# One transformer layer with routed experts, one core: the g2 row on VectorE, the first loads reordered, and g2's broadcast buffer lent to an expert load

## The chip, the cores and the metric

One core of a Trainium2 chip runs the program. It has five engines with queues of their own: TensorE (PE in the profile; its weight loads are PEld), VectorE (DVE), ScalarE (ACT), GpSimd (POOL) and SyncE (SP), which here only issues DMAs. The metric is device microseconds (us) of one execution, the median of several.

## The reference, cut to what matters

One layer of a decoder on 256 tokens of width 2048. A conditioning vector `c` gives six rows of 2048 numbers, `mod = silu(c) @ ada_w + ada_b`, split into `sh1, sc1, g1, sh2, sc2, g2`. Then

```
h = rmsnorm(x) * norm1_g * (1 + sc1) + sh1
x = x + g1 * (mixer(h))          # w_in (2048 x 5392), attention, gated delta rule, w_out (2048 x 2048)
h = rmsnorm(x) * norm2_g * (1 + sc2) + sh2
x = x + g2 * (moe(h))            # 32 experts, two per token; each a gated MLP 2048 -> 512 -> 2048
out = rmsnorm(x) * final_norm_g
```

All in float32. The weights are some 570 MB, each read once.

## The kernel before, in words

**Loads.** Every weight comes in pieces of 128 x 2048 float32 (1 MB, 8 KB in each partition) through one `Stream`, called `st` (its `pump`, `done` and `grow` are lines 122 to 160). The stream has a list of loads in a fixed order and a set of slots, tiles named `ring`. A load is issued on SyncE's queue into the next free slot; when a piece has been used, `done` frees its slot for the next load of the list. `grow` adds slots, `retire` takes a slot out once its present load has been used. At the start there are five slots (`main`, three, and `side`, two) and four borrowed ones (`spare`), which go back at the end of the w_in stage. When the buffers of the mixer are closed, four more come (`rb`), after the second half of w_out three (`rd`) and two (`yh`, `yl`, for one load each), and after routing two (`h20`, `h21`).

**The order of work.** The program is written in one order; a planner that simulates the engines then sets the order of the instructions on each engine, keeping the dependences. The stages are:

1. Start (lines 166 to 241). `c` is loaded and turned into columns. The conditioning rows sc1 and sh1 are made in slices (`ada_tile`, products on PE into a bank named `prow`). Before any product with w_in can run, x must be in, its mean square known (squares on ScalarE, line 518; reciprocal root; spread over columns as `rb`, line 529), and the modulated transpose `hx` made (lines 321 to 350) from `mod`, which needs small rows of `norm1_g` and `ada_b` (`crow`). SyncE issues x (four loads), then the five slots of the ring, then six small loads and the 128 KB of `wbr` (line 225), then the four spare slots.
2. w_in, by slices of its rows (`win_tile`, `win_pair`). Each piece is split into a high and a low part (`split`: ScalarE casts, line 289; VectorE or GpSimd subtracts, line 290) and three products are made of them.
3. The fill: attention and the delta rule (`delta`, `attention`), with w_in's last columns and the rows g1, sh2, sc2, g2 laid between them by `tick`. A row takes 16 pieces of ada_w (`row_tile`, lines 424 to 453). For g1, sh2 and g2 (i = 0, 1, 3) PE makes four products of 512 columns per piece, into a bank `prow`; for sc2 (i = 2) VectorE multiplies the piece by its column of silu(c) and adds it to a running sum `racc`, two instructions of 128 x 1024 per piece (line 441; the first piece line 439), and four products at the end sum over partitions. The results are added to `mrow` (line 450).
4. w_out in two halves (`wout_part`, four parts each). The first eight pieces of g2's row are read in the fill, the last eight in the first half, two after each part. In the second half each part also spreads 512 columns of g2 over the partitions (two products with `identr`, a copy by ScalarE, line 1036) into `g2b`, a tile of 8 KB per partition that lives to the end.
5. Routing (lines 1052 to 1154): a chain of short VectorE instructions from the logits to the one-hot matrices `oh`.
6. The experts, two at a time. For each, eight pieces of gate and up weights (`hidden`: products `u` on PE) and four of down weights (`second`: products `d`, then VectorE scales by the gate and `g2b`, line 1232). `scatter` adds the result to x. 384 pieces in all.
7. The final norm and the stores.

Of the kernel before, what the change touches and what calls it, by code (L numbers as in the profile page):

```python
# [50 lines left out]
def hybrid_moe(ctx: ExitStack, tc: tile.TileContext, x, c, norm1_g, norm2_g, early, ada_w, ada_b, w_bb,  # L51
# [118 lines left out]
    cols, crows, start_loads = {}, {}, []  # L170
    for nk, r in ((4, 4), (2, 8)):
        w = P * nk
        rows = crows[nk] = tmp.tile([P, 2, 256], F32, name="crow", tag="ct", bufs=2).rearrange("p u t -> p (u t)")[0:3 * r, 0:w]
        for i, row in enumerate((norm1_g[0, 0:r * w], ada_b[0, 0:r * w], ada_b[0, D:D + r * w])):
            start_loads.append((rows[i * r:(i + 1) * r], row.rearrange("(j n) -> j n", n=w)))
# [43 lines left out]
    spare = [(wk, "Tm"), (wk, "qk"), (cst, "h20"), (cst, "h21")]  # L219
    for n in range(4):  # L220
        nc.sync.dma_start(x1[n], xin[n])
    st.grow(*main, *side)
    wbr = tmp.tile([P, 2, 384], F32, name="wbr", tag="pT").rearrange("p u s -> p (u s)")[:, 0:16 * KT]
    for a in start_loads + [(wbr, w_bb)]:
        nc.sync.dma_start(*a)
    st.grow(*spare)

    for nk, r in ((4, 4), (2, 8)):
# [6 lines left out]
        for k0, n in SLICES:  # L235
# [4 lines left out]
           .bitcast(F32R).rearrange("p (k n) -> p k n", n=16) for i in range(2)]  # L240
    wbr = wbr.rearrange("p (k n) -> p k n", n=16)
# [50 lines left out]


# [130 lines left out]
    def row_tile(i, kt):  # L424
        def on_pe(t):
            if kt == 0:
                rowp[i] = bank("r", name="prow2")
            for g in range(4):
                mm(rowp[i][32 * g:32 * g + 32, :], csil[:, kt, 3 - i:35 - i], t[:, 512 * g:512 * (g + 1)],
                   start=(kt == 0), stop=(kt == 15))  # L430

        def on_dve(t):
            if kt == 0:
                rowp[i] = wk.tile([P, D], F32, name="racc", tag="racc")
            acc = rowp[i]
            for h in range(2):
                c = slice(1024 * h, 1024 * (h + 1))
                if kt == 0:
                    V.tensor_scalar(acc[:, c], t[:, c], csil[:, kt, 3:4], None, op0=ALU.mult)
                else:  # L440
                    V.scalar_tensor_tensor(acc[:, c], t[:, c], csil[:, kt, 3:4], acc[:, c], op0=ALU.mult, op1=ALU.add)
            if kt == 15:
                rowp[i] = bank("d", name="prow2")
                for g in range(4):
                    mm(rowp[i][32 * g:32 * g + 32, :], onec[:, 3 - i:35 - i], acc[:, 512 * g:512 * (g + 1)])

        def f(t):
            (on_dve if i == 2 else on_pe)(t)
            if kt == 15:
                V.tensor_tensor(mrow, mrow, rowp.pop(i), op=ALU.add)  # L450
                if i == 2:
                    V.scalar_tensor_tensor(n2row, mrow, 1.0, n2row, op0=ALU.add, op1=ALU.mult)
        return f
# [76 lines left out]
    S.copy(wbb[0], wbr)  # L530
    V.tensor_tensor(wbb[1], wbr, wbb[0], op=ALU.subtract)
# [476 lines left out]
    g2b = ring2.tile([P, D], F32, name="g2b")  # L1008
# [22 lines left out]
    for n in range(4):  # L1031
        ns = slice(512 * n, 512 * (n + 1))
        wout_part(n, (1, 2), g1hl, ep.tile([P, 512], F32, name="g1s", tag="ak0"))
        pg = bank("w")
        spread2(pg, g1hl, 3, n)
        S.copy(g2b[:, ns], pg)
# [4 lines left out]
        for b in range(NB):  # L1041
# [8 lines left out]
            S.activation(y, x1[n][:, b], AF.Square, accum_out=ss2[:, b, n:n + 1])  # L1050
    r2 = cst.tile([P, NB], F32, name="r2")
# [22 lines left out]
    g2h = g2b.rearrange("p (n h j) -> p n h j", n=4, h=2)  # L1074
# [141 lines left out]
    def second(u, hT, gs, ys, st, n0, m, yl=None, at=None):  # L1216
# [13 lines left out]
        for h, q in ((u, slice(0, 64)), (1 - u, slice(64, 128))):  # L1230
            o = z[q, 0:256 * m] if yl else ys[h][q, c]
            V.scalar_tensor_tensor(o.rearrange("p (n j) -> p n j", n=m), pd[q, 0:256 * m].rearrange("p (n j) -> p n j", n=m),  # L1232
                                   gs[q, h, u:u + 1], g2h[q, n0:n0 + m, h], op0=ALU.mult, op1=ALU.mult)
# [69 lines left out]
    behind = []  # L1303
    for e in range(0, NE, 2):
# [8 lines left out]
        hid.append(hidden(2 * a + 1, now.xg, st))  # L1313
# [166 lines left out]
```

## Time and profile before

| | us |
|---|---|
| median of three runs | 1624.28 (1623.28 to 1625.85) |
| the profiled execution | 1624.69 |
| its span, first to last instruction | 1622.9 |

The page gives the busy time of each engine (PE 1521.0, DVE 732.8, ACT 400.4, POOL 184.0), the span in 40 slices, the DMA queues, the chain that ended last, and the costliest groups of instructions with the idle time before them and what ended it. The trace can be asked for instructions in order of time, for the busy time of any stretch, and for waits. Busy time of PE is modelled for pipelined products: a PE that is shown busy all through may still have room; the starts of its weight loads (PEld) show how densely it issues. A row like `473.48 1.86 PEld ... x16 [0.84 <-issue]` says that 16 weight loads began at 473.48 us, after 0.84 us in which PE issued nothing and no semaphore is known to have held it.

### The profile page before, as it was taken

Reading aid. Unit: us, or ns where it says so; the run is one execution under the profiler, and the core shown is the slowest. Engines: PE = TensorE matmul, PEld = TensorE weight load, DVE = VectorE, ACT = ScalarE, POOL = GpSimd, SP = SyncE. Lnnn points to the kernel's source line nnn. Section 1 sums busy time; section 2 is a strip of 40 time slices with the busy share of each in tenths; the row PEclk is TensorE's granted clock in tenths of the full one; section 3 lists DMA queues with packets and bytes.
Section 4 is the critical chain, followed back from the end, with each engine's and each line's share of the span. In section 5 each row is a group of like instructions: output and inputs, shape, how many; then the busy total and the mean of one; then the engine's idle time right before and its main releaser. Section 6 shows DMA issues by size and latency. Waiting matters only on the chain. (4 is left out here: it accounts for less than half of the span.)

```text
span 1622.9 us, 23431 instructions
## 1 busy us (share of the span) xinstructions
PE 1521.0 (94%) x9852; PEld 926.3 (57%) x9852; DVE 732.8 (45%) x1201; ACT 400.4 (25%) x691; POOL 184.0 (11%) x103
## 2 busy tenths in 40 slices
PE   5999999999999999899999999999999999999895
PEld 3778877678776677445445445455445435445433
DVE  3544587487624544333443443344235225325325
ACT  4333366444443344120110110111011101101103
POOL 1111223234333241000000000000000000000001
PEclk8999999999999999899999999999999999999998
DMA  9977654888857374799999999999999999999995
GB/s 377 408 300 290 216 224 178 349 316 320 312 216 291 144 305 180 281 410 420 392 420 420 421 421 420 421 420 420 420 421 421 420 421 421 421 420 420 422 420 223
DMA packets 81412, 573.74 MB, mean 354 GB/s; under 512 B 9740, under 2 KB 10100, under 8 KB 12312
## 3 DMA queue, kind: packets, MB, share of 16 engines
q1 hardware_dynamic: 81272, 572.20, 87.4%
q8 instruction: 79, 1.29, 0.3%
q14 instruction: 29, 0.24, 0.0%
q10 hardware_dynamic: 32, 0.01, 0.0%
HBM read 570.07 MB, written 2.10 MB: 353 GB/s over the span
## 5 line engine op out<-in xcount | busy, mean ns | idle before, releaser
L67 PE MATMUL u<-ring,xg 128*64 128x512 f32 x2048 | 483.7, 602 | 7.5 <-DMA ring<-in_expert_gu_dram 7.3
L67 PEld LDWEIGHTS u<-ring,xg 128*64 128x64 f32 x2048 | 134.4, 136 | 235.7 <-issue 190.7
L67 PE MATMUL d<-ring,hidT 128*64 128x256 f32 x2048 | 239.1, 384 | 12.0 <-DMA ring<-in_expert_dn_dram 8.6
L67 PE MATMUL w<-hx,stg 128*128 128x256 f32 x1440 | 191.0, 288 | 7.4 <-ACT hx L349 2.8
L67 PEld LDWEIGHTS d<-ring,hidT 128*64 128x64 f32 x2048 | 144.1, 137 | 93.1 <-issue 10.6
L67 PEld LDWEIGHTS w<-hx,stg 128*128 128x128 f32 x1440 | 177.9, 191 | 32.8 <-issue 10.9
L290 POOL TENSOR_TENSOR stg<-ring,stg 128x1024 fp32r<-128x1024 f32 x50 | 121.9, 2439 | 373.0 <-ACT stg L289 273.4
L289 ACT CAST stg<-ring 128x1024 fp32r<-128x1024 f32 x116 | 121.3, 1047 | 164.3 <-PE w L67 140.9
L1248 DVE TENSOR_TENSOR xt<-xt,s 128x512 f32<-128x512 f32 x120 | 82.5, 687 | 159.2 <-PE s L67 158.4
L1235 ACT CAST yh<-z 64x512 fp32r<-64x512 f32 (+1 forms) x132 | 78.8, 597 | 279.2 <-DVE z L1232 274.3
L1232 DVE SCALAR_TENSOR_TENSOR z<-d,gs,g2b 64x512 f32<-64x512 f32 (+1 forms) x132 | 95.8, 726 | 84.0 <-PE d L67 81.8
L290 DVE TENSOR_TENSOR stg<-ring,stg 128x1024 fp32r<-128x1024 f32 x66 | 91.4, 1385 | 65.2 <-ACT stg L289 65.0
L67 PE MATMUL prow<-ring,csil 128*32 128x512 f32 (+1 forms) x768 | 102.3, 565 | 13.8 <-DMA ring<-in_early_dram 13.5
L1337 POOL TENSOR_TENSOR xf<-xt,fgb 128x1024 f32<-128x1024 f32 x3 | 7.0, 2359 | 953.1 <-DVE xf L1232 953.1
L1165 DVE TENSOR_TENSOR xg<-g,sh2c 128x512 f32<-128x512 f32 x64 | 43.6, 690 | 136.8 <-PE u L67 76.2
L67 PEld LDWEIGHTS s<-yh,wt 128*128 128x128 f32 x240 | 45.4, 189 | 96.4 <-issue 60.4
L1204 ACT ACTIVATE hid<-u 64x512 f32<-64x512 f32 x32 | 18.9, 590 | 317.4 <-PE u L67 300.8
L1236 DVE TENSOR_TENSOR yl<-z,yh 64x512 fp32r<-64x512 f32 (+1 forms) x132 | 87.3, 661 | 5.1 <-ACT yh L1235 1.5
L67 PE MATMUL s<-yh,wt 128*128 128x256 f32 x240 | 75.6, 335 | 9.1 <-ACT yh L1235 5.0
L67 PE MATMUL w<-stg,hx 128*128 128x256 f32 x576 | 81.1, 291 | 0.7 <-DVE ak L271 0.7
L1205 DVE TENSOR_TENSOR hid<-hid,u 64x512 f32<-64x512 f32 x32 | 22.1, 690 | 129.8 <-ACT hid L1204 129.6
L67 PEld LDWEIGHTS w<-stg,hx 128*128 128x128 f32 x576 | 71.1, 189 | 13.2 <-issue 9.8
(396 smaller groups left out, 1590.4 us busy)
## 6 DMA issues: line engine op xcount, KB each, us to landing
ring<-in_expert_gu_dram SPq DMA_DIRECT2D x256, 1024.0 KB, 19.8
ring<-in_expert_dn_dram SPq DMA_DIRECT2D x128, 1024.0 KB, 19.8
ring<-in_early_dram SPq DMA_DIRECT2D x90, 1024.0 KB, 8.2
ring<-in_ada_w_dram SPq DMA_DIRECT2D x64, 1024.0 KB, 6.4
xt<-in_x_dram SPq DMA_DIRECT2D x8, 512.0 KB
out_dram<-xt SPq DMA_DIRECT2D x8, 256.0 KB, 3.9
fgb<-in_final_norm_g_dram SPq DMA_DIRECT2D x1, 1024.0 KB
rw<-in_router_w_dram SPq DMA_DIRECT2D x1, 320.0 KB, 5.1
```

The lines of the kernel that those rows point to most:

```text
L67: return T.matmul(o, lhsT, rhs, start=start, stop=stop, skip_group_check=True)
L289: S.copy(hi, src)
L290: (G if nsplit[0] % GS[part] == GS[part] - 1 else V).tensor_tensor(lo, src, hi, op=ALU.subtract)
L1165: V.tensor_tensor(self.xg[:, 2 * q:2 * q + 2, 0:w], p[:, 0:2 * w].rearrange("p (k s) -> p k s", k=2), sh2c.rearrange("p n k -> p (n k)")[: ...
L1204: S.activation(hid[64:128], p[0:64], AF.Silu)
L1205: V.tensor_tensor(hid[0:64], hid[64:128], p[64:128], op=ALU.mult)
L1232: V.scalar_tensor_tensor(o.rearrange("p (n j) -> p n j", n=m), pd[q, 0:256 * m].rearrange("p (n j) -> p n j", n=m), gs[q, h, u:u + 1], g2h ...
L1235: S.copy(ys[h][q, c], o)
L1236: V.tensor_tensor(yl[h][q, c], o, ys[h][q, c], op=ALU.subtract)
L1248: V.tensor_tensor(x1[n][:, b], x1[n][:, b], p, op=ALU.add)
L1337: G.tensor_tensor(xf[n // 2][:, n % 2], x1[n], fgb[:, None, 512 * n:512 * (n + 1)].to_broadcast([P, NB, 512]), op=ALU.mult)
```

## The change

Three things are changed.

- The start. The five slots of the ring are filled first, then the four loads of x are issued, then the four spare slots. The six small rows and `wbr` are issued on ScalarE's queue, the rows at the very start, into buffers named `t2`; the split of `wbr` into its two halves is written earlier.
- g2's row. Its 16 pieces take the path that sc2's take: 32 instructions on VectorE into `racc`, and four products at the end.
- g2's spread. The tile `g2b` is no longer filled in the second half of w_out. After that half its slot is given to the stream for one load and then retired; during the second expert the tile is made in the same place and filled by `spread_g2`, four times two products and one copy, one after each of the last four pieces of that expert. The high and low halves of the row are made before routing ends, in the two buffers of `z`.

```
@@ start
+        rows = crows[nk] = scratch(w, 3 * r)
+        S.dma_start(rows[0:r], norm1_g[0, 0:r * w].rearrange("(j n) -> j n", n=w))
...
+    st.grow(*main, *side)
     for n in range(4):
         nc.sync.dma_start(x1[n], xin[n])
-    st.grow(*main, *side)
-    wbr = tmp.tile([P, 2, 384], F32, name="wbr", tag="pT").rearrange("p u s -> p (u s)")[:, 0:16 * KT]
-    for a in start_loads + [(wbr, w_bb)]:
-        nc.sync.dma_start(*a)
     st.grow(*spare)
...
+    S.dma_start(wbr, w_bb)
...
+    S.copy(wbb[0], wbr)
+    V.tensor_tensor(wbb[1], wbr, wbb[0], op=ALU.subtract)
@@ row_tile
-            (on_dve if i == 2 else on_pe)(t)
+            (on_dve if i >= 2 else on_pe)(t)
@@ second half of w_out
-        pg = bank("w")
-        spread2(pg, g1hl, 3, n)
-        S.copy(g2b[:, ns], pg)
...
+    st.grow((ring2, "g2b"))
+    st.retire((ring2, "g2b"))
@@ experts
+    g2hl = halves(*(mp.tile([P, 512], F32R, name="g2hl", tag="z") for _ in range(2)), mrow)
+    def spread_g2(n):
+        if n == 0:
+            assert not any(x == (ring2, "g2b") for _, x in st.tiles)
+            g2t.append(ring2.tile([P, D], F32, name="g2b", tag="g2b"))
+        p = bank("s", 1)
+        spread2(p, g2hl, 3, n)
+        S.copy(g2t[0][:, 512 * n:512 * (n + 1)], p)
...
-        hid.append(hidden(2 * a + 1, now.xg, st))
+        hid.append(hidden(2 * a + 1, now.xg, st, [] if e else [lambda: None] * 4 + [lambda n=n: spread_g2(n) for n in range(4)]))
```

## Rows read from the trace of the kernel before

**Rows 1.** The page of the profile: its first line, and of the 40 slices of the span (40.6 us each) the granted clock of PE and the busy share of the DMA engines, in tenths.

```profile
span 1622.9 us, 23431 instructions
...
PEclk8999999999999999899999999999999999999998
...
DMA  9977654888857374799999999999999999999995
```

**Rows 2.** Busy time by stretch (start:end, length, busy us and instructions of each engine, granted clock, share of the 16 DMA engines, GB/s), in the expert stage: its first long stretch (those after it up to 1580 read the same: share 1.01, 420 to 421 GB/s).

```profile
760.00:1000.00 240.00, 232.26 (x1418) 117.61 (x1419) 93.56 (x144) 27.38 (x45) 0.00 (x0) 0.99 1.01 415
```

**Rows 3.** The same view in stretches of 5 us, around the start of the expert stage.

```profile
625.00:630.00 5.00, 5.00 (x22) 3.53 (x20) 4.40 (x7) 2.51 (x6) 0.02 (x1) 1.00 0.00 0
...
655.00:660.00 5.00, 2.43 (x10) 2.33 (x11) 2.79 (x14) 0.00 (x0) 0.00 (x0) 0.50 0.96 400
...
660.00:665.00 5.00, 5.00 (x28) 4.64 (x28) 1.69 (x3) 1.39 (x2) 0.00 (x0) 0.64 0.04 11
...
695.00:700.00 5.00, 5.00 (x26) 2.29 (x24) 1.56 (x11) 0.20 (x1) 0.00 (x0) 1.00 1.02 433
```

**Rows 4.** Instructions in order of time (start, length, engine, line, operation, tensors, count, idle time before it and what ended it), SyncE's queue of DMA issues in the first 35 us.

```profile
2.62 2.44 SPq L186 DMA_DIRECT2D ring<-in_early_dram  x5
...
20.52 11.55 SPq L186 DMA_DIRECT2D ring<-in_early_dram  x11
```

**Rows 5.** Busy time by stretch of 4 us in the first 30 us.

```profile
0.00:4.00 4.00, 0.28 (x1) 0.18 (x1) 1.68 (x8) 1.59 (x2) 1.60 (x9) 1.00 0.54 165
...
8.00:12.00 4.00, 1.36 (x16) 0.68 (x16) 0.98 (x5) 2.94 (x8) 0.00 (x0) 1.00 1.01 428
...
20.00:24.00 4.00, 3.36 (x34) 2.40 (x35) 1.12 (x4) 0.78 (x2) 0.00 (x0) 1.00 0.66 223
```

**Rows 6.** Instructions in order of time, all engines, between the squares of x and the first products with w_in.

```profile
8.75 0.61 ACT L518 ACTIVATE t<-xt 128x512 f32<-128x512 f32 x1
...
11.21 0.48 DVE L526 TENSOR_SCALAR t<-ident,rs 128x128 f32<-128x128 f32 x2
...
25.52 1.99 ACT L289 CAST stg<-ring 128x1024 fp32r<-128x1024 f32 x2 [3.21 <-DMA ring<-in_early_dram]
...
26.60 1.23 DVE L290 TENSOR_TENSOR stg<-ring,stg 128x1024 fp32r<-128x1024 f32 x1 [2.70 <-ACT stg L289]
...
27.74 0.15 DVE L321 TENSOR_TENSOR mod<-d,cols 128x4 f32<-128x4 f32 x1
...
31.24 7.86 PE L67 MATMUL w<-hx,stg 128*128 128x256 f32 x48
```

**Rows 7.** What PE waited for between 31 and 100 us (the whole answer: us in total, times, longest).

```profile
PE w L67 <- ACT hx L349: 2.8, 1, 2.8
PE w L67 <- DVE hx L350: 0.5, 1, 0.5
```

**Rows 8.** Costliest groups between 440 and 580 us: PE's products for the rows on TensorE (busy us, mean ns of one). Of these 136 records 8 belong to another row and 128 to g2's (64 products, two records each).

```profile
L67 PE MATMUL prow<-ring,csil 128*32 128x512 f32 x136 | 22.1, 602 | 0.3 <-DMA ring<-in_ada_w_dram 0.3
```

**Rows 9.** Weight loads on PE in order of time: the first, one of the middle and the last of the fourteen bursts of g2's products, each with the row that follows it.

```profile
459.32 0.15 PEld L67 LDWEIGHTS prow<-ring,csil 128*32 128x32 f32 x6
460.31 0.74 PEld L67 LDWEIGHTS d<-t,Um 128*128 128x128 f32 x6 [0.84 <-DVE stg L290]
...
522.82 0.16 PEld L67 LDWEIGHTS prow<-ring,csil 128*32 128x32 f32 x8 [0.33 <-issue]
524.50 0.97 PEld L67 LDWEIGHTS d<-t,Um 128*128 128x128 f32 x8 [1.52 <-PE prow L67]
...
566.99 0.14 PEld L67 LDWEIGHTS prow<-ring,csil 128*32 128x32 f32 x4 [0.25 <-issue]
567.97 0.30 PEld L67 LDWEIGHTS w<-stg,aq 128*128 128x128 f32 x2 [0.84 <-issue]
```

**Rows 10.** The instructions that touch racc, the running sum of the sc2 row, which VectorE keeps today (count: shortest/median/longest ns, first and last start), and PE's weight loads that close such a row, with the row that follows.

```profile
L441 DVE SCALAR_TENSOR_TENSOR racc<-ring,csil,racc x30: 1255/1276/3402, 317.2 to 432.9; 128x1024 f32<-128x1024 f32 x30
```

```profile
455.55 0.16 PEld L67 LDWEIGHTS prow<-racc,onec 128*32 128x32 f32 x8
456.54 0.52 PEld L67 LDWEIGHTS a<-kswap,cq 64*128 64x128 f32 x4 [0.84 <-issue]
```

**Rows 11.** Busy time of all engines from 440 to 570 us, and of line 290 (the splits) alone.

```profile
440.00:570.00 130.00, 124.35 (x777) 89.21 (x777) 55.41 (x85) 48.93 (x92) 39.74 (x21) 0.97 0.61 227
```

```profile
440.00:570.00 130.00, 13.27 (x9) 22.39 (x9) 0.97 0.61 227
```

**Rows 12.** VectorE and GpSimd in order of time, two pairs: line 852 alone and line 852 beside a GpSimd split.

```profile
316.57 0.69 DVE L852 TENSOR_TENSOR Um<-ident,Um 128x512 f32<-128x512 f32 x1
...
322.85 2.51 DVE L852 TENSOR_TENSOR Um<-ident,Um 128x512 f32<-128x512 f32 x1
```

```profile
322.00 2.81 POOL L290 TENSOR_TENSOR stg<-ring,stg 128x1024 fp32r<-128x1024 f32 x1
```

**Rows 13.** Weight loads on PE around the first of the four spreads of g2 in the second half of w_out.

```profile
587.59 3.09 PEld L67 LDWEIGHTS w<-stg,bv 128*128 128x128 f32 x14 [0.36 <-issue]
591.04 0.29 PEld L67 LDWEIGHTS w<-g1hl,identr 32*128 32x128 f32 x2 [0.36 <-issue]
591.70 2.17 PEld L67 LDWEIGHTS w<-stg,bv 128*128 128x128 f32 x10 [0.36 <-issue]
```

**Rows 14.** PE in order of time in the routing stage: its wait for VectorE.

```profile
656.79 1.03 PE L67 MATMUL t<-Ae,before 128*128 128x32 f32 x4 [6.46 <-DVE Ae L1107]
```

More of the change, by code (lines that the diff above doesn't have):

```diff
@@ L168, in hybrid_moe @@
     S.dma_start(craw, c[0].rearrange("(k p) -> k p", p=P))
-    cols, crows, start_loads = {}, {}, []
+    cols, crows = {}, {}
     for nk, r in ((4, 4), (2, 8)):
         w = P * nk
-        rows = crows[nk] = tmp.tile([P, 2, 256], F32, name="crow", tag="ct", bufs=2).rearrange("p u t -> p (u t)")[0:3 * r, 0:w]
-        for i, row in enumerate((norm1_g[0, 0:r * w], ada_b[0, 0:r * w], ada_b[0, D:D + r * w])):
-            start_loads.append((rows[i * r:(i + 1) * r], row.rearrange("(j n) -> j n", n=w)))
+        rows = crows[nk] = scratch(w, 3 * r)
+        S.dma_start(rows[0:r], norm1_g[0, 0:r * w].rearrange("(j n) -> j n", n=w))
+        S.dma_start(rows[r:2 * r], ada_b[0, 0:r * w].rearrange("(j n) -> j n", n=w))
+        S.dma_start(rows[2 * r:3 * r], ada_b[0, D:D + r * w].rearrange("(j n) -> j n", n=w))
     V.memset(csil, 0.0)
@@ L240, in hybrid_moe @@
            .bitcast(F32R).rearrange("p (k n) -> p k n", n=16) for i in range(2)]
+    wbr = tmp.tile([P, 2, 384], F32, name="wbr", tag="pT").rearrange("p u s -> p (u s)")[:, 0:16 * KT]
+    S.dma_start(wbr, w_bb)
     wbr = wbr.rearrange("p (k n) -> p k n", n=16)
@@ L529, in hybrid_moe @@
     V.tensor_copy(rb, pt[:, 0:256])
-    S.copy(wbb[0], wbr)
-    V.tensor_tensor(wbb[1], wbr, wbb[0], op=ALU.subtract)
     use(first[3:CP])
@@ L1007, in hybrid_moe @@
     st.grow(*slots(ring2, "rb", R2))
-    g2b = ring2.tile([P, D], F32, name="g2b")
     h2hi, h2lo = ([ring2.tile([P, D], F32R, name=f"{n}{b}") for b in range(NB)] for n in ("h2hi", "h2lo"))
@@ L1073, in hybrid_moe @@
     psum = ctx.enter_context(tc.tile_pool(name="mps", bufs=1, space=bass.MemoryType.PSUM, reuse_waits="tile"))
-    g2h = g2b.rearrange("p (n h j) -> p n h j", n=4, h=2)
+    g2hl = halves(*(mp.tile([P, 512], F32R, name="g2hl", tag="z") for _ in range(2)), mrow)
+    g2t = []
     def small(name, shape, dt=F32):
@@ L1232, in second @@
             V.scalar_tensor_tensor(o.rearrange("p (n j) -> p n j", n=m), pd[q, 0:256 * m].rearrange("p (n j) -> p n j", n=m),
-                                   gs[q, h, u:u + 1], g2h[q, n0:n0 + m, h], op0=ALU.mult, op1=ALU.mult)
+                                   gs[q, h, u:u + 1], g2t[0].rearrange("p (n h j) -> p n h j", n=4, h=2)[q, n0:n0 + m, h], op0=ALU.mult, op1=ALU.mult)
             if yl:
```

## The prediction

> **What bounds the kernel now.** I read the page first, then stretches, then single waits. The page's DMA row says 9 almost throughout from the eighteenth slice on and much less before it [rows 1]. In the expert stage the stretch view shows the 16 DMA engines at a share of 1.01 [rows 2]: they never rest, so one piece (1.049 MB at 420 GB/s) costs 2.50 us whatever the engines do. In stretches of 5 us that state begins near 695 us [rows 3]. Before it the DMA engines pause: 0.00 at 625 to 630 us and 0.04 at 660 to 665 us, with PE shown busy all through. There every slot of the ring is full and PE decides when one comes free. So the end is the time at which the DMA engines become saturated, plus the bytes left over 420 GB/s, plus a tail that the change doesn't touch. Two things shorten it: a microsecond less on PE's path before 695 us counts once, and a piece brought in during a pause counts 2.50 us.
>
> PE's path reaches far back. From 31 to 100 us PE's products waited 3.3 us in all, none of it for a load [rows 7]. Its clock stands at 8 or 9 tenths in all slices [rows 1], so there is little to win from that.
>
> The sums are made against the profiled execution, 1624.69 us (span 1622.9 and 1.8 around it), 0.4 above the median of the runs.
>
> **The start.** PE's first product with w_in is at 31.24 us [rows 6]. It was not x that was late: the last squares began at 8.75 and the roots were spread by 11.69 (11.21 and 0.48). It was the first piece of w_in. It is sixth in the list (five pieces of ada come first), so it has the first spare slot, and SyncE issues that only at 20.52, behind the small loads and `wbr` [rows 4]; the DMA engines stood at 0.66 from 20 to 24 us against 1.01 before [rows 5]. The cast of that piece waited 3.21 us for it, and its subtraction (26.60 to 27.83) sat ahead of `mod` on VectorE; from `mod` (27.74) to the first product passed 3.50 us [rows 6].
>
> After the change five pieces and x, 5.24 + 2.10 = 7.34 MB, come first. At 428 GB/s [rows 5] that is 17.2 us, and with the 2 us that the DMA engines lose in the first 4 (share 0.54) x is there at 19 to 20 us. One more square (0.61) and the chain from the squares to the roots (9.36 to 11.69, 2.33 us) [rows 6] give 23; the same 3.50 us give 26.5. The first w_in piece lands 1.05 MB after x, near 22, and its cast and subtraction (1.99 + 1.23) end at 25.2. That is 4.7 us sooner than 31.24. The small loads on ScalarE's queue cost its idle time only, as long as x is what ScalarE waits for. Ends: +5 if all of that comes, -2 if x, which now has no slack, is late and the subtraction again goes ahead of `mod` (that order cost 3.6 us). I take 3, since the work on VectorE is the same and only one of the two delays is surely gone. By rows 7 there is no load wait behind it that would swallow the gain.
>
> **g2's row.** PE gives up 64 products, 128 records of the 136 that took 22.1 us [rows 8]. What they hold of PE's issue is read from the weight loads: from the first load of a burst to the next other load. There are fourteen bursts, 0.99 us in the first (459.32 to 460.31), 0.98 in the last (566.99 to 567.97), 19.7 us in all [rows 9]. Eight of them, 9.6 us, lie between attention and delta products until 492; three, 5.4 us, in the tail of the delta rule (510 to 525), where PE waits for VectorE anyway: after that at 522.82 PE still idled 1.52 us [rows 9]. Of these I count the last at nothing and half of the rest, 1.8. The three in the first half of w_out, 4.7 us, count fully. Against them stand four closing products, 0.99 us by those of sc2's row [rows 10]. Net 9.6 + 1.8 + 4.7 - 1.0 = 15.1 us.
>
> VectorE takes 32 instructions of 1.276 us, 40.8 us [rows 10]. From 440 to 570 us it is busy for 55.4 of 130 [rows 11], so they fit: 96 of 130. But the queue is in order. Behind each sit subtractions whose result PE needs, and a piece's slot is free only when both of its instructions are done; SyncE's queue is in order too, so everything behind that slot waits, w_out's pieces included. Some 85 VectorE instructions run in that window [rows 11]; each finds a row instruction ahead with a chance of 41/130 and waits half of 1.28 us, 0.2 us, together 17 us. Four staging buffers stand between VectorE and PE; I let a quarter, 4 us, through. So 11 us. Ends: 15 (none gets through) and -25 (all 40.8 us in PE's way, the 15.1 saved).
>
> The row shows a second price. Line 852 takes 0.69 us alone and 2.51 us when a GpSimd subtraction (322.00 to 324.81) runs beside it [rows 12]; of the 32 existing row instructions the longest took 3.40 us [rows 10]. The Trainium skill, SBUF — State Buffer, section "Who interferes with whom", says that a VectorE instruction with two inputs in SBUF and a GpSimd instruction that reads SBUF share one read interface, and whichever comes second is held until the first is through; rows 12 agree. By that rule the row's gain is what the first rival below makes of it. The median of 1.276 says that most row instructions escape it.
>
> **g2's spread and its buffer.** In w_out's second half each spread holds PE's issue from 590.68 (587.59 + 3.09) to 591.70, 1.02 us, of which 0.1 would be spent anyway [rows 13]. Four times 0.9 is 3.6 us on a PE that is busy throughout (ends 2 and 4.1). The same products now run in the second expert, near 695 us, when the DMA engines are the limit: nothing, and if that cover failed, the same 3.6 back.
>
> The lent slot lets one more piece in while the DMA engines would pause (660 to 665 us, 0.04 [rows 3]): 2.5 us. Ends 0 (its issue comes in order behind loads that wait for the routing) and 2.5. The new halves of the row put one VectorE instruction of 512 columns, about 0.69 us as line 852 [rows 12], near the routing chain, for which PE waits 6.46 us [rows 14]. I take 0.5 lost, ends 0 and 1.
>
> **Sum.** 3 + 11 + 3.6 + 2.5 - 0.5 = 19.6 us; 1624.69 - 19.6 = 1605.1, against the median 1604.7. I say 1605.
>
> **Rivals.**
> One: VectorE and GpSimd hold each other up. GpSimd is busy 39.7 us of the 130, nine splits of 22.4 us among it [rows 11]. If each of the nine waits for a whole row instruction (1.28), 11.5 us come back on the path of PE, and the row gives nothing net. Then 3 + 3.6 + 2.5 - 0.5 = 8.6, that is 1616. For: rows 12. Against: the median of rows 10.
>
> Two, slower: the row makes VectorE the bound. It has 130 - 55.4 = 74.6 us free there. At 3.40 us each 32 instructions need 109 and the stage grows by 34; less the other parts' 8.6 the kernel would stand near 1650, at a mean of 3.0 (96) at 1637. It decides from 32 d = 74.6 + 8.6, a mean d of 2.6 us. For: some run at twice the median, and SyncE's queue passes a late slot on to all loads. Against: the median, and that VectorE is free more than half of the time.
>
> Three: the start and the slot don't do what they say: x's lateness takes the place of the late w_in piece, and the lent slot's load is issued too late. Then 11 + 3.6 - 0.5 = 14.1, 1610.6. For: -2 to 5 at the start is wide. Against: rows 4 and 5.
>
> Four: everything comes at its better end but for what cannot: 4.7 + 15.1 + 3.6 + 2.5 = 25.9, 1599. For: VectorE's free time. Against: its in-order queue.
>
> Five: the planner lays the engines' order anew and loses elsewhere what is won: 1624.
>
> **How the numbers follow.** The forecast 0.37 (its own range 1601 to 1609), rival one 0.18, two 0.13, three 0.15, four 0.10, five 0.07. 0.2%, 3.2 us, is about what a measurement of this kernel can tell from no change. Faster: 0.37 + 0.18 + 0.15 + 0.10 = 0.80; same 0.07; slower 0.13. The range holds the forecast and rivals one, three and four with some room, 1594 to 1622; it leaves out rivals two and five, 0.20.
>
> **What would show it.** Right: the first w_in product near 27 us; no `prow` products after the g1 and sh2 rows but two closing groups of four; 32 more instructions at line 441 with a mean under 1.6 us; the second half of w_out shorter by 3 to 4 us; the DMA engines saturated some 20 us sooner than 695; 420 GB/s from there on. Wrong: PE waiting for `stg` from VectorE or GpSimd between 455 and 570; a mean over 2 us at line 441; SyncE waiting for `racc`; the first w_in product at 31 us or later; a stage of experts that isn't shifted but stretched.

## The result, and the profile after

The changed kernel takes 1634.29 us (median of six runs, 1630.63 to 1636.18), the kernel before, on the same chip, 1624.53 (1623.26 to 1626.68). The ratio is 1.0058, 95% interval [1.0048, 1.0068]: slower by 9.4 us. The forecast was 1605 with a range of 1594 to 1622, and 0.13 for slower. The execution that was profiled is the slowest of the six, 1636.18.

The page of the changed kernel, its first line, the granted clock and the DMA share of the 40 slices, to be read beside [rows 1]:

```profile
span 1634.4 us, 23238 instructions
...
PEclk8999999999998899799999999999999999999998
...
DMA  9987564888766374799999999999999999999995
```

The clock has a new dent in the thirteenth and fourteenth slices (490 to 572 us), within the stretch where the time went. I followed landmarks through both traces. The first product with w_in came later (31.24 to 33.31 us), the closing products of sc2's row earlier (455.55 to 454.81). From there to the high half of the g1 row, the first thing behind the first half of w_out, the kernel before took 124.8 us (455.55 to 580.30) and the changed one 136.5 (454.81 to 591.3). Of those 11.7 us it won 2.3 back by the first one-hot matrix of the routing, and lost 2.8 from there to the end. These are single executions; what the parts are worth is taken from the runs below.

Busy time by stretch (length, busy us and instructions of PE, PEld, DVE, ACT and POOL, granted clock, DMA share, GB/s), first of the kernel before, then of the changed one.

```profile
460.00:480.00 20.00, 20.00 (x154) 13.91 (x151) 6.20 (x14) 8.77 (x23) 5.82 (x3) 1.00 0.71 257
480.00:500.00 20.00, 20.00 (x162) 16.05 (x161) 6.26 (x8) 9.81 (x15) 8.61 (x4) 1.00 0.97 378
...
520.00:540.00 20.00, 15.82 (x72) 11.82 (x73) 16.08 (x25) 4.72 (x8) 3.47 (x4) 0.83 0.40 152
```

```profile
460.00:480.00 20.00, 17.67 (x147) 16.45 (x146) 20.00 (x21) 7.71 (x20) 5.18 (x3) 1.00 0.74 267
480.00:500.00 20.00, 14.26 (x103) 11.89 (x102) 20.00 (x18) 11.46 (x20) 14.10 (x4) 0.98 1.01 410
520.00:540.00 20.00, 11.27 (x34) 8.28 (x33) 16.79 (x25) 2.90 (x5) 2.59 (x3) 0.58 0.31 106
...
760.00:1000.00 240.00, 231.48 (x1378) 117.87 (x1374) 92.81 (x145) 27.38 (x45) 0.00 (x0) 0.98 1.00 407
```

For 40 us VectorE has no gap at all, where it had been busy for 12.5, and PE, which had been busy throughout, is idle for 8. From 520 to 540 us PE works 11.3 us of 20 instead of 15.8, and its granted clock is 0.58 instead of 0.83, close to the lower of its two levels (1.2 of 2.4 GHz). The last line answers to [rows 2]: 407 GB/s against 415.

What PE and SyncE waited for between the two landmarks in the changed kernel (engine, line, releaser: total, times, longest):

```profile
PE w L67 <- POOL stg L291: 6.9, 6, 4.3
PE w L67 <- DVE stg L291: 6.4, 2, 4.4
PE d L67 <- DVE t L909: 6.2, 2, 5.5
...
SPq L190 <- DVE racc L444: 23.3, 5, 8.4
```

All of these stood in the prediction's list of what would show it wrong, but for the third: PE waits 6.2 us for a step of the delta rule.

### The profile page after: what moved, and what is told of

Same layout as the page of the kernel before. It is cut to its first block, busy times and chain, and to the rows that moved or that the text cites. A ratio compares the mean times of both kernels' runs of the same rounds, so it can differ in the third digit from the quotient of the medians.

```text
span 1634.4 us, 23238 instructions
## 1 busy us (share of the span) xinstructions
PE 1515.8 (93%) x9732; PEld 933.5 (57%) x9732; DVE 774.0 (47%) x1234; ACT 401.4 (25%) x693; POOL 188.5 (12%) x103
## 5 line engine op out<-in xcount | busy, mean ns | idle before, releaser
L1166 DVE TENSOR_TENSOR xg<-g,sh2c 128x512 f32<-128x512 f32 x64 | 43.7, 690 | 126.4 <-PE u L67 71.1
L444 DVE SCALAR_TENSOR_TENSOR racc<-ring,csil,racc 128x1024 f32<-128x1024 f32 x60 | 87.7, 1494 | 7.7 <-DMA ring<-in_ada_w_dram 7.7
L67 PE MATMUL prow<-ring,csil 128*32 128x512 f32 (+1 forms) x640 | 82.0, 553 | 0.3 <-DVE csil L182 0.3
```

Of the source, the lines that this page charges most:

```text
L67: return T.matmul(o, lhsT, rhs, start=start, stop=stop, skip_group_check=True)
L1166: V.tensor_tensor(self.xg[:, 2 * q:2 * q + 2, 0:w], p[:, 0:2 * w].rearrange("p (k s) -> p k s", k=2), sh2c.rearrange("p n k -> p (n k)")[: ...
```

## The experiments

Each kernel was timed in five rounds beside the kernel before. "us" is the ratio less 1, times the median of the kernel before beside it (1624.5 to 1626.0); an interval reaches 1.3 to 2.5 us to either side. The expectations were reckoned from medians, which differ from these by up to 1.5 us.

| run | what is in it | median | ratio, 95% interval | us |
|---|---|---|---|---|
| e3 | the new start alone | 1619.89 | 0.9973 [0.9964, 0.9982] | -4.4 |
| e2 | g2's row on VectorE alone | 1637.35 | 1.0080 [1.0065, 1.0096] | +13.0 |
| e4 | late spread and lent slot alone | 1626.52 | 1.0012 [1.0003, 1.0020] | +2.0 |
| e1 | all but the row | 1626.44 | 1.0007 [0.9997, 1.0017] | +1.1 |
| e5 | pieces 0 to 7 of the row on VectorE | 1623.38 | 0.9991 [0.9980, 1.0001] | -1.5 |
| e6 | pieces 8 to 15 | 1635.36 | 1.0061 [1.0049, 1.0074] | +9.9 |
| e13 | pieces 8 to 11 | 1628.36 | 1.0020 [1.0010, 1.0029] | +3.3 |
| e14 | pieces 12 to 15 | 1634.88 | 1.0052 [1.0039, 1.0066] | +8.5 |
| e9 | VectorE loaded, no slot held | 1634.29 | 1.0051 [1.0037, 1.0064] | +8.3 |
| e12 | e6, splits on GpSimd | 1634.51 | 1.0054 [1.0041, 1.0068] | +8.8 |
| e7 | spread written late, no slot | 1623.41 | 0.9987 [0.9978, 0.9997] | -2.1 |
| e16 | late spread, g2's room lent, yl's not | 1621.42 | 0.9984 [0.9975, 0.9994] | -2.6 |
| e15 | one load fewer | 1630.19 | 1.0022 [1.0013, 1.0031] | +3.6 |
| e8 | start, spread in the routing | 1619.82 | 0.9969 [0.9958, 0.9980] | -5.0 |
| e10 | start, pieces 0 to 7 | 1618.97 | 0.9968 [0.9957, 0.9979] | -5.2 |
| e11 | e10, spread in the routing | 1618.25 | 0.9952 [0.9939, 0.9966] | -7.8 |
| e17 | e10, spread written late, no slot | 1619.02 | 0.9967 [0.9955, 0.9979] | -5.4 |

### The three parts, one by one

e1 is the changed kernel with one line back, e2 the kernel before with that line:

```
-            (on_dve if i >= 2 else on_pe)(t)      # e1; e2 the other way round
+            (on_dve if i == 2 else on_pe)(t)
```

e3 takes the hunks of the start alone, e4 those of w_out and of the experts.

> The changed kernel with g2's row back on TensorE (only sc2's on VectorE); start and lent slot as changed. Theory (the row on VectorE costs some 11.7 us, by the landmarks between the closing products of sc2's row and the casts of the g1 row, and start and slot nearly cancel): 1634.3 - 11.7 = 1622.6, and the cast of the g1 row comes back from 591.3 to about 580. Rival (the row is worth what was forecast, and the planner's new order that came with the start and the late spread is what costs): 1634 or more, the g1 cast near 590.

> The kernel before with g2's row on VectorE and nothing else. Theory (the row alone costs 11.7 us): 1624.5 + 11.7 = 1636, SyncE waiting for racc for some 60 us, the g1 cast near 592. Rival (the row gains as forecast, the rest of the change loses): 1614 to 1620.

> The kernel before with the new start alone. Theory (the start reaches its first w_in product 2.1 us later but makes it up to 0.7 to 1.7 us ahead by 200 to 450 us, and that is kept): 1624.5 - 1 = 1623.5. Rival (the late first product is what counts, and the lead came from elsewhere): 1626.5 or more.

> The kernel before with the late spread of g2 and the lent slot alone. Theory (w_out's second half gains 2.4 us, and the spreads inside the second expert hold back its down products, so that slots come free late and the DMA engines pause near 780 and 840 us, which costs 3 us): 1625, with two stretches of 10 us below a DMA share of 0.92 between 770 and 860. Rival (the pauses in the changed kernel come from the late arrival of the row's stage, not from the spread): no such pauses, 1624.5 - 2.4 - 2.5 = 1619.6.

The row is what makes the kernel slow: +13.0 alone, 8.3 beside the rest (9.4 less 1.1). The start gains more than its landmarks had said. The slot and the late spread together lose 2.0. The three parts add up to 10.6, near the 9.4 measured, but start and slot together (e1, +1.1) are 3.5 worse than their sum. So the theory for e1, that they nearly cancel and leave 1622.6, was too low by 3.8.

**How the start gains.** e3 in order of time: the issue of x, its last square, the spread of the roots, the modulation, the first product with w_in.

```profile
8.76 8.08 SPq L223 DMA_DIRECT2D xt<-in_x_dram  x4
...
22.14 0.61 ACT L521 ACTIVATE t<-xt 128x512 f32<-128x512 f32 x1
...
24.93 0.79 PE L67 MATMUL d<-t,ones 128*128 128x128 f32 x2 [6.91 <-DVE t L529]
...
30.51 0.88 DVE L350 SCALAR_TENSOR_TENSOR t<-d,mod,rb 128x256 f32<-128x256 f32 x2
...
31.59 2.67 PE L67 MATMUL w<-hx,stg 128*128 128x256 f32 x19
```

The last square ended at 22.75, where I had worked out some 20.6, and from the spread of the roots (24.93) to the modulation passed 5.6 us: PE, at half clock behind its idle time of 6.91 us, had four transposes of x and twelve products of the ada rows in between. So the first product was no sooner than before (31.24). But what followed later was. The two fences are stretches of 8 us, of the kernel before and of e3:

```profile
32.00:40.00 8.00, 8.00 (x63) 7.31 (x61) 6.39 (x18) 3.54 (x5) 0.87 (x3) 0.78 1.01 427
88.00:96.00 8.00, 5.70 (x33) 3.56 (x34) 4.43 (x9) 1.71 (x4) 1.17 (x1) 0.79 1.01 419
```

```profile
32.00:40.00 8.00, 8.00 (x74) 7.05 (x74) 7.79 (x22) 3.75 (x6) 0.96 (x3) 1.00 1.01 420
88.00:96.00 8.00, 6.92 (x56) 5.46 (x57) 3.44 (x8) 1.95 (x4) 1.20 (x1) 1.00 0.84 344
```

The full clock from 32 to 40 us is not the start's doing: in the traces of the twelve kernels with the old start it is 0.76 to 1.00 there, in the seven with the new one 0.82 to 1.00. What all seven share against all twelve is the stretch near 90 us. There PE waits 1.1 us for `hx` instead of 2.8, and from 88 to 96 us its clock is 1.00, with the old start 0.57 to 0.79. At 95 us e3 leads by 2.6 us, at the closing products of sc2's row near 455 by 3.2, at the end of the profiled execution by 5.8.

Single executions scatter widely even so. Up to 450 us the seven kernels have the same order of instructions on PE, VectorE and ScalarE, and the twelve have theirs; yet the closing products start at 452.2 to 454.8 us in the seven (middle value 454.5) and at 454.9 to 461.0 in the twelve (457.8). The middle values are 3.4 us apart. Part of the scatter goes with the clock: in the changed kernel, e1, e11 and e17 it was 0.50 from 24 to 32 us, and the first product was at 33.1 to 33.3; in e3, e8 and e10 it was 0.66 to 0.68, and the first product at 31.4 to 31.6.

### Where the row's price lies

e5 and e6 move half of the row, e13 and e14 a quarter; the rest goes on PE as before. Each part has its own first and last product and its own addition to `mrow`, which this cut leaves out (e13 and e14 pick the pieces from a list, to the same effect):

```
-            (on_dve if i == 2 else on_pe)(t)
+            (on_dve if i == 2 or i == 3 and kt < 8 else on_pe)(t)     # e6: kt >= 8; e13: 8 to 11; e14: 12 to 15
```

> The kernel before, with only the first eight pieces of g2's row (those read between attention and delta rule) on VectorE and the last eight on TensorE. The whole row on VectorE cost 11.7 us (1637.35 against 1625.66). Theory (each half costs by itself, as the landmarks split it: 4.7 us ahead of the transposes that follow the delta rule, 7 us in the first half of w_out): 1625.7 + 4.7 = 1630.4. Rival (only the sum of both overfills VectorE's queue; eight pieces find room): within 2 us of 1625.7, or faster by TensorE's saved products, down to 1618.

> The kernel before, with only the last eight pieces of g2's row (two after each part of the first half of w_out) on VectorE. Theory (slots of the ring are held until VectorE has done with them, so w_out's next piece is late and TensorE idles): 1625.7 + 7 = 1632.7, with SyncE waiting for racc between 540 and 580 us. Rival (only the sum of both halves overfills VectorE's queue): within 2 us of 1625.7, or faster, down to 1621.

> The kernel before with pieces 8 to 11 of g2's row alone on VectorE (they come while the delta rule ends, 500 to 527 us). Theory (they stand in VectorE's queue ahead of a step of the delta rule for which TensorE waits; in the run with pieces 8 to 15 TensorE waited 6.2 us there instead of 0.6, and the transposes after it came 2.1 us later against the closing products): 1625 + 2 to 5, that is 1627 to 1630. Rival (the price lies in w_out's first half alone): 1623 to 1625.5.

> The kernel before with pieces 12 to 15 of g2's row alone on VectorE (they come after the first and second part of w_out's first half, 553 to 581 us). Theory (two times a split that TensorE needs stands behind three row instructions and two of the sums, TensorE idles 4 us and runs at half clock after it; in the run with pieces 8 to 15 this stage lost 7.5 us): 1625 + 6 to 8, that is 1631 to 1633. Rival (the price is that of the delta rule's end alone): 1624 to 1626.

The split by landmarks was wrong for the first half: it costs nothing (-1.5, its interval touches zero). The whole row costs 4.6 more than its halves (13.0 against 8.4). The traces place this ahead of the transposes behind the delta rule (line 952). From the closing products of sc2's row to there pass 80 to 81 us with none of the row on VectorE, 79.2 to 79.3 with its first half (e5, e10, e11, e17), 83.2 with pieces 8 to 15 or 8 to 11 (e6, e13), but 85.7 and 85.9 with all of it (the changed kernel and e2). The price lies in three places, two of them in the second half.

The first place is the end of the delta rule (e13, +3.3). VectorE and, in the last line, PE of the changed kernel there; e13 looks the same:

```profile
518.00 3.59 DVE L444 SCALAR_TENSOR_TENSOR racc<-ring,csil,racc 128x1024 f32<-128x1024 f32 x2
521.51 0.67 DVE L926 TENSOR_TENSOR ob<-ob,d 128x512 f32<-128x512 f32 x1
522.11 1.27 DVE L444 SCALAR_TENSOR_TENSOR racc<-ring,csil,racc 128x1024 f32<-128x1024 f32 x1
523.30 0.68 DVE L908 TENSOR_TENSOR t<-d,egc 128x512 f32<-128x512 f32 x1
523.91 1.27 DVE L444 SCALAR_TENSOR_TENSOR racc<-ring,csil,racc 128x1024 f32<-128x1024 f32 x1
525.10 0.68 DVE L910 TENSOR_TENSOR ob<-d,egc 128x512 f32<-128x512 f32 x1
525.70 0.68 DVE L909 TENSOR_TENSOR t<-vtok,t 128x512 f32<-128x512 f32 x1
...
526.52 2.05 PE L67 MATMUL d<-t,Um 128*128 128x128 f32 x8 [5.50 <-DVE t L909]
```

Four row instructions stand between and ahead of four short steps, the last of which (line 909) PE waits for. PE has nothing else left (its `prow` products, which filled this gap before, are gone) and idles 5.50 us, where it had waited 0.64 at the same step; its eight products then take 2.05 us instead of 1.13.

The second place is the first half of w_out (e14, +8.5). VectorE and PE of e14, and two stretches of 5 us there:

```profile
550.08 1.42 DVE L442 TENSOR_SCALAR racc<-ring,csil 128x1024 f32<-128x1024 f32 x2 [3.91 <-DMA ring<-in_ada_w_dram]
...
551.41 1.29 DVE L980 TENSOR_TENSOR w<-w,g1s 128x512 f32<-128x512 f32 x2
...
552.61 2.47 DVE L444 SCALAR_TENSOR_TENSOR racc<-ring,csil,racc 128x1024 f32<-128x1024 f32 x2
555.00 1.22 DVE L290 TENSOR_TENSOR stg<-ring,stg 128x1024 fp32r<-128x1024 f32 x1
...
556.27 0.80 PE L67 MATMUL w<-stg,aq 128*128 128x512 f32 x1 [4.64 <-DVE stg L290]
...
557.29 1.05 PE L67 MATMUL w<-stg,aq 128*128 128x512 f32 x2
...
550.00:555.00 5.00, 1.62 (x6) 1.01 (x6) 4.92 (x7) 0.20 (x1) 0.00 (x0) 1.00 0.51 170
555.00:560.00 5.00, 3.73 (x9) 2.96 (x10) 2.41 (x4) 0.00 (x0) 0.00 (x0) 0.56 0.85 303
```

VectorE first waits 3.91 us, in order, for the row's piece to land; only then come the row instructions, the sums, more row instructions, and at 555.00 the subtraction that PE needs. PE idles 4.64 us. Then its clock falls: a pair of products takes 1.05 us, which took 0.63 just before (547.79 in e14), until past 562 us. From 548 to 564 us the stage loses some 6 us against the kernel before, in this one place, and that after the 1.92 us that PE's products for the row had taken there.

The third place shows only with the whole row. VectorE, GpSimd and PE of the changed kernel:

```profile
487.91 8.30 POOL L939 TENSOR_TENSOR tok<-tok,dng 128x1024 f32<-128x1024 f32 x2 [1.34 <-ACT tok L938]
491.28 6.01 DVE L444 SCALAR_TENSOR_TENSOR racc<-ring,csil,racc 128x1024 f32<-128x1024 f32 x2
...
496.16 3.33 POOL L291 TENSOR_TENSOR stg<-ring,stg 128x1024 fp32r<-128x1024 f32 x1
...
499.55 0.80 PE L67 MATMUL w<-stg,cq 128*128 128x512 f32 x1 [4.30 <-POOL stg L291]
```

The two products of GpSimd take 8.30 us here, in the kernel before 2.37 and 2.40 (489.80 and 495.43); the two row instructions beside them take 3.0 us each. The subtraction that PE needs comes behind all this, takes 3.33 us itself (2.39 in e12 at 553.00), and PE idles 4.30 us. At the same step of e2 it is 2.73; all that PE waits for subtractions of GpSimd between 455 and 545 us is 0.2 us in e5 and nothing in e6. This is rival one of the prediction, on PE's path.

Is it VectorE's queue, or the slots of the ring that are held until VectorE has read a piece? e9 leaves the row on PE and loads VectorE for pieces 8 to 15 with as much work, on a tile of zeros; e12 takes w_out's subtractions out of VectorE's queue:

```
+            one = rowp["one"][:, kt - 8:kt - 7]                # e9, for i == 3 and kt >= 8
+            S.copy(one, t[:, 0:1])
+            for h in range(2):
+                c = slice(1024 * h, 1024 * (h + 1))
+                V.scalar_tensor_tensor(rowp["x"][:, c], rowp["x"][:, c], one, rowp["x"][:, c], op0=ALU.mult, op1=ALU.add)
...
-GS = (3, 2, 2)                                                # e12, on top of e6
+GS = (3, 2, 2, 1)
-                w = split(t[:, k:k + 2], 2, 2)
+                w = split(t[:, k:k + 2], 2, 3 if qs[0] == 0 else 2)
```

> The kernel before, g2's row on TensorE throughout; in addition VectorE gets, for each of the row's last eight pieces, two instructions of 128 x 1024 that multiply and add a tile of zeros and do not read the piece (they start when ScalarE has copied one column of it), so no slot of the ring waits for VectorE. The output is not changed. The second half of the row on VectorE cost 9.4 us (1635.36 against 1625.93) although it spared TensorE 4.7. Theory (VectorE's in-order queue puts those instructions ahead of w_out's splits, TensorE waits for the splits, and its clock falls to half for some microseconds after): 1625.9 + 9.4 + 4.7 = 1640, at least 1634. Rival (the price is the slots that are held until VectorE has done): under 1629.

> The second half of the row on VectorE (1635.4), with all sixteen subtractions of w_out's first half on GpSimd, so that none of them waits in VectorE's queue behind a row instruction. Theory (the waits for those subtractions are the price): no wait for stg from VectorE in that stage, 1622 to 1628. Rival (VectorE and GpSimd hold each other up, or the held slots): 1635 or more.

e9 costs 8.3 us without holding a slot, so held slots are not needed for a price of this size. Its trace doesn't show it at both places, though: the stretch from the closing products of sc2's row to the transposes behind the delta rule is 6.1 us longer, while w_out's first half costs nothing. There PE still had `prow` products to fill with. So e9 doesn't exclude held slots for the second place; what speaks against them is that PE's 4.64 us there ended with a subtraction on VectorE and not with a load. PE's saved products seem worth little: e6 saves them and costs no less than e9, though in another place.

e12 was a miss: 1634.5 where I expected 1622 to 1628. VectorE and GpSimd there:

```profile
556.67 10.49 DVE L441 SCALAR_TENSOR_TENSOR racc<-ring,csil,racc 128x1024 f32<-128x1024 f32 x4
...
559.49 3.25 POOL L290 TENSOR_TENSOR stg<-ring,stg 128x1024 fp32r<-128x1024 f32 x1 [1.28 <-ACT stg L289]
...
562.91 3.17 POOL L290 TENSOR_TENSOR stg<-ring,stg 128x1024 fp32r<-128x1024 f32 x1 [0.17 <-ACT stg L289]
```

The long waits for subtractions are gone, as the theory said (0.5 us is the longest left), but four row instructions now take 10.49 us, 2.62 on average, where e14 has two in 2.47; GpSimd's subtractions take 3.2 instead of the 2.39 that one takes beside no row instruction (at 553.00 in the same run). The row ends so late that PE waits 4.6 us for it at its closing products. That is rival one again: the two engines hold each other up. Still, clearing the queue was worth something: from the transposes to the casts of the g1 row pass 47.3 us, against 50.8 in e6 and 43.7 in the kernel before. e12 lost that again ahead of the transposes (85.5 us against e6's 83.2). The Trainium skill, SBUF — State Buffer, "Who interferes with whom", gives the rule (one read interface for a GpSimd instruction and a VectorE instruction with two inputs in SBUF), and here the trace agrees. In the changed kernel, of the row's 32 instructions the 12 that ran beside one of GpSimd's took 1.96 us on average, the other 20 1.25 (worked out from the starts and lengths of both); all of them came to 1.51.

### The spread and the lent slot

e7 writes the spread late but lends nothing; e16 lends g2's room and leaves out yl's, so that as many loads as before lie ahead; e15 is the kernel before with yl's room not lent; e8 is e3 with the spread after w_out:

```
-    st.grow((ring2, "g2b"))                      # e7, from e4
-    st.retire((ring2, "g2b"))
...
-    for t in ("yh", "yl"):                       # e15, from before; e16, from e4
+    for t in ("yh",):
...
+    for n in range(4):                           # e8, ahead of the routing, from e3
+        p = bank("s", 1)
+        spread2(p, g2hl, 3, n)
+        S.copy(g2b[:, 512 * n:512 * (n + 1)], p)
```

> The kernel before with g2's spread moved into the second expert, but its tile kept free until then, so no load is lent its room. Spread and lent slot together gave 1626.5. Theory (the late spread spoils the order of the first experts, and the slot gains nothing): 1626.5 or more. Rival (the one load more that is in the ring spoils it): 1625.7 - 2.4 = 1623.3, by the gain in w_out's second half.

> Late spread and g2's room lent, but the room of yl not lent: as many loads ahead of the experts as in the kernel before. With both rooms lent it was 1626.5, with the late spread and no lent room of g2 1623.4. Theory (a load more spoils the experts): 1623.4, within 1.5 us. Rival (it is the lent room itself, or the order that the planner lays with it): 1626.5 or more.

> The kernel before with one load fewer ahead of the experts (the room of yl is not lent for one load). Theory (TensorE bounds the kernel as far as the last pause of the DMA engines, at 770 to 790 us, by when the ring is full whether or not one load came sooner): 1625, within 1.5 us. Rival (the step of the prediction: a piece that comes in during a pause is worth 2.5 us): 1627.5.

> The new start alone (1619.9) with g2's spread moved out of w_out's second half to the end of that half, where TensorE waits for the routing; no slot is lent, g2's row stays on TensorE. Theory (what TensorE gives up in w_out's second half counts, if the spread lies in an idle stretch): 1619.9 - 2.4 = 1617.5. Rival (TensorE bounds the first experts as well, so moving the products earns nothing, or the planner lays the experts anew): 1619.9 or more.

e7 did not become what its expectation calls it. Its tile is free from the start, so the planner laid all four spreads into the routing, as e8 has them. With g2's room lent (e4, e16, e1 and the changed kernel) the first spread's two products are in the routing as well and the other three spreads in the first experts. PE of e7 and of e16:

```profile
655.31 1.21 PE L67 MATMUL s<-g2hl,identr 32*128 32x512 f32 x2 [0.68 <-ACT g2b L1308]
657.88 1.22 PE L67 MATMUL s<-g2hl,identr 32*128 32x512 f32 x2
663.48 1.22 PE L67 MATMUL s<-g2hl,identr 32*128 32x512 f32 x2
```

```profile
699.82 0.72 PE L67 MATMUL s<-g2hl,identr 32*128 32x512 f32 x2
706.16 0.72 PE L67 MATMUL s<-g2hl,identr 32*128 32x512 f32 x2
```

So the late spread is worth 2.6 (e16), with the spread in the routing 2.1 (e7); both lie below the 3.6 forecast and within its ends of 2 and 4.1. One load more, with the spread late in both, costs 4.6 (e4 less e16), where 2.5 was to be gained. One load fewer costs too (e15, +3.6; its rival's 2.5 lies within the interval of 2.1 to 5.0), so my theory for that run, that TensorE bounds the kernel up to 790 us and a load counts nothing, fell as well. The count of loads does not settle it; where the DMA engines pause does. Summed from the trace's DMA packets, the time at which so many MB were still to be moved, against the kernel before (single executions again: e16's is the fastest of its eleven, 2.7 below its median, e15's 3.1 below):

| MB left (us in the kernel before) | e3 | e1 | e4 | e16 | e15 | changed |
|---|---|---|---|---|---|---|
| 380 (697.4) | -4.5 | -6.9 | -4.3 | -3.5 | +3.6 | +6.3 |
| 350 (768.7) | -4.6 | -4.3 | -2.4 | -3.6 | +3.6 | +8.4 |
| 340 (795.3) | -5.7 | -0.8 | -0.6 | -6.0 | +2.8 | +8.8 |
| 320 (842.9) | -5.8 | +1.2 | +1.2 | -6.0 | +2.7 | +11.0 |
| 290 (914.2) | -5.6 | +2.5 | +2.6 | -5.9 | +3.5 | +13.0 |
| 50 (1484.9) | -5.6 | +2.5 | +2.6 | -5.9 | +3.5 | +13.0 |

From 914 us to the last loads near 1590 nothing moves any more; that is the stretch in which the DMA engines alone set the time. (In the tail behind it e1, e15 and the changed kernel win 1.1 to 1.5 back.) Before it, e1, e4 and the changed kernel lose their lead in steps, near 700 to 770, 770 to 795, 820 to 840 and 890 to 910. The kernel before pauses once in 770 to 790 us (two stretches of 10 us), e16 has no stretch of 10 us under 400 GB/s from 700 us to the tail. One such step in e4, PE's products of `scatter` with what they waited for, and two stretches of 10 us; then the same two of e16:

```profile
817.84 0.38 PE L67 MATMUL s<-yh,wt 128*128 128x256 f32 x1 [0.78 <-DVE xt L1248]
819.36 0.39 PE L67 MATMUL s<-yh,wt 128*128 128x256 f32 x1 [0.78 <-DVE xt L1248]
821.17 0.58 PE L67 MATMUL s<-yh,wt 128*128 128x256 f32 x1 [0.78 <-DVE xt L1248]
823.06 1.87 PE L67 MATMUL t<-Ge,oh 128*128 128x2 f32 x8 [0.68 <-ACT wt L1179]
...
820.00:830.00 10.00, 7.77 (x36) 5.39 (x37) 2.65 (x5) 1.18 (x2) 0.00 (x0) 0.51 1.02 422
830.00:840.00 10.00, 10.00 (x88) 5.73 (x84) 6.17 (x9) 2.47 (x4) 0.00 (x0) 1.00 0.90 337
```

```profile
820.00:830.00 10.00, 8.30 (x68) 5.16 (x66) 6.17 (x9) 2.46 (x4) 0.00 (x0) 0.89 1.02 422
830.00:840.00 10.00, 10.00 (x66) 5.13 (x64) 6.31 (x9) 2.46 (x4) 0.00 (x0) 0.94 1.01 416
```

`scatter` has one bank, so each of its products waits 0.78 us for VectorE to add the one before. Between other products that is hidden. In e4 several stand one behind another, from 816 to 826 us; no piece of the ring is used for 10 us, the clock falls to 0.51, and in the next stretch the DMA engines move 337 GB/s, as no slot had come free. The order is the planner's, laid anew for each kernel. e15 has such a chain too (from 741 to 749 us). Nor does it take a load more: e7's profiled execution, the slowest of its twelve (1629.74, median 1623.41), pauses near 780, 840 and 890 to 910 us too. How much of the slot's 4.6 us is this order, and whether a load more would be worth anything in an unchanged order, stays open: it can't be told apart while the planner lays the order.

e8 equals e3 within the intervals (1619.82 and 1619.89): the spread in the routing's idle time earned nothing that can be told.

### Together

e10, e11 and e17 put together what had gained:

```
# e10: e3 and e5;  e11: e8 and e5;  e17: e3, e5 and e7
```

> The new start with the first half of g2's row on VectorE, the second on TensorE, the spread where it was. Theory (both parts add, since TensorE's path bounds the kernel as far as the last pause of the DMA engines in the expert stage): 1619.9 - 2.5 = 1617.4. Rival (the half row's gain was the scatter of the runs): 1619.9.

> The new start, the first half of the row on VectorE, and the spread moved to the routing. Theory (the spread's place earns nothing, as found): the same as the run without it, 1617.4. Rival (the spread in the routing's idle time counts): 1615.

> The new start, the first half of g2's row on VectorE, the spread inside the second expert with its room kept free. Theory (the late spread's 2.5 us add to the 1619.0 of the other two): 1616.5. Rival (they don't add, as the start's gain did not add to the lent slot): 1619 or more.

e17 is no test of the late spread: its tile is free early, as in e7, and the planner laid its spreads into the routing. On every engine its instructions and SyncE's loads stand in the same order as e11's. So the 2.4 us between e11 (-7.8 [-9.9, -5.5]) and e17 (-5.4) are scatter between two measurements of one schedule, and e11 can't be called the best of the three. Against e3 none of e10, e11 and e17 is clearly better, so most of it is the start; all are 15 to 17 us below the changed kernel. Whether the late spread adds to the start without a load more was not run. With the slot the two did not add up, as e1 said.

## Why the prediction was wrong

**The bound** was read rightly in kind and wrongly in place. "In stretches of 5 us that state begins near 695 us": the DMA engines did move 420 GB/s from 695 to 770, and then paused. The long row of [rows 2] has 415 GB/s and a share of 1.01 over 240 us, and two stretches of 10 us in it, 330 and 391 GB/s, vanish in that mean. So PE's work in the first experts was still on the path, and the cover that I had given to the spread's new place and to the order was not there.

**The start**, -3: -4.4 measured. The sign held, the size lies near its better end of 5. The way was another: the first product was not at 26.5 but at 31.59, since x was later than worked out, the modulation did not follow the roots at once (PE's products between them were left out of the sum), and PE's clock was low after its idle time. The lead that is there came near 90 us and behind it, which no term of the sum had; that the number came near is luck.

**g2's row**, -11: +13.0. This is the step that failed, and within it two things. The first is the term for VectorE's queue, "let a quarter, 4 us, through". I took 85 instructions that each wait half a row instruction and let four staging buffers absorb most. The waits were few and long instead: several row instructions in a row ahead of the one instruction for which PE had nothing else to do. In the changed kernel PE idled 5.50, 4.42 and 4.30 us in three places (4.64 in e14 at the second). The second is the credit for PE's saved products. In e5, where VectorE had room, w_out's first product came 3.68 us sooner (495.07 to 491.39) though that execution had been 3.1 behind at the closing products. Of these 6.8 us some 3 are only that the planner had put 23 products of the delta rule behind that landmark; so some 4 of the 9.6 us were won by then. At the transposes 1.8 were left (79.26 us from the closing products instead of 81.08). PE now waits 1.64 us instead of 0.64 for a step of the delta rule on VectorE, which ends when it ends, and its clock over the stretch is 0.89 instead of 0.96 (0.89 in e10, e11 and e17 too, 0.98 in e3). I had allowed for that wait in three bursts of the tail, and not for the eight ahead of it.

Rival two had the sign and the engine, not the mechanism: it decided from a mean of 2.6 us per instruction, and the mean was 1.51. VectorE was busy 101.4 of 136.5 us. It was not its throughput that bound, but its order. Rival one, the mutual hold-up, is real and costs some 8 us of VectorE's time (32 times 1.51 less 1.25). How much of that was on the path is not shown, but the 4.30 us at 495 us were. None had the clock: around PE's idle times of 4.30, 5.50 and 4.42 us the clock stood at the lower level for some 3, 17 and 7 us.

**The spread**, -3.6: -2.6 without a load more (e16). **The lent slot**, -2.5: +4.6. "A piece brought in during a pause counts 2.50 us" holds only if no pause follows, and here one did. Rival five, that the planner lays the order anew and loses elsewhere, is what was seen in the expert stage; I had given it 0.07.

## What to carry to other kernels

Before an engine with idle time is given work, look for the instructions on it for which the critical engine waits with nothing else to do, and ask how many of the new ones can stand in a row ahead of them; the mean load says little. When a planner lays the order, look in the trace where it put the instructions before you read a run as a test of their place. Work that is taken from the critical engine ahead of a wait whose end another chain sets is not won. A share near 1 over a long stretch is no proof of saturation: the last pause decides from where a transfer-bound stage starts, and all that lies ahead of it still counts by the compute engine's order.

## What the runs showed of the hardware

After idling 4.64 us PE ran pairs of products in 1.05 us that took 0.63 just before, with a granted clock of 0.56 in that stretch of 5 us and 0.76 in the next. So a wait can cost PE more than its length: here some 6 us for 4.64, although 1.92 us of products had gone from that place. And executions of the same order of instructions differed by 1.9 us at the first product with w_in (31.41 in e10, 33.31 in the changed kernel), by when the clock came back. VectorE and GpSimd slowed each other down: two GpSimd products that took 2.37 and 2.40 us took 8.30 together beside row instructions, and these 3.0 us each instead of 1.25.
